# A two-block model on one core: the steps round the recurrences' gates and between states, values and first scores in another order

## The chip, the core and the metric

The kernel runs on one core of a Trainium2 chip. A core has TensorE (matmuls into PSUM; its weight loads are shown apart), VectorE, ScalarE, GpSimd and SyncE, each with a queue of its own that it works off in order, and shares of 16 DMA engines. Here SyncE only issues transfers; ScalarE and GpSimd issue some too. The metric is the device time of one execution in microseconds, as the median of several runs.

## The reference

Two model blocks are applied to x of shape (1, 512, 1024), all in fp32.

```
first block:   h = rmsnorm(x);  p = h @ w_in -> lru_x, lru_gate, four_in
               c = depthwise conv of lru_x over time
               two gated linear recurrences over c (forward, backward):
                 a = exp(8 r log_sigmoid(lam)),  h_t = a_t h_(t-1) + sqrt(1-a^2) i c
               y = concat(gelu(lru_gate) * (h_f + h_b), fft2 of four_in)
               x = x + y @ w_out
               x = x + expert-choice MoE(rmsnorm(x)): 16 experts, 64 rows each, FF 2048
               x = rmsnorm(x)
second block:  h = rmsnorm(x);  h @ w_in -> q, k, v, z_a, u, z_s, g_a, g_s
               y_a = (banded attention with relative bias(q, k, v) * silu(z_a)) @ w_attn_out
               y_s = diagonal state space model of u, 32 groups, 64 states each;
                     gelu, GLU, * silu(z_s), @ w_ssm_out
               x = rmsnorm(x + (sigmoid(g_a) * y_a + sigmoid(g_s) * y_s) @ w_out)
```

## The kernel before

The order of all instructions is written out by hand: each engine runs its instructions in the order in which the code issues them, and semaphores make it wait for operands and for buffers. Most matmuls take fp32 operands as a pair of a rounded high part and a low part: `Pair.put` (lines 107 and 108, or 110 and 111 with a scale) copies the high part on ScalarE and subtracts it on VectorE or GpSimd, and `mm3` (lines 121 to 123) runs high by high, high by low, low by high. A projection of one weight unit is 24 matmuls.

The dense weights come in units of 512 KB through `Stream`: `load` (line 140) has SyncE fetch a unit into half of one of two raw buffers, `work` splits it into one of three pair buffers, with the low part on GpSimd or, for every third unit, on VectorE, and then calls `load` again; `get` hands out a unit and works ahead so that two more lie split. A raw buffer holds a pair of units, so a load into it waits until both of its units have been split. SyncE's queue is worked in order, so what is issued behind such a load waits too.

First block, start. SyncE loads xT (x transposed) in five transfers, the first two weight units, x in four blocks `xs`, two more units, a table of constants with the identity, the gate weights `bd`, the DFT table, and two further units. `half` and `part` split the first two units and xT's eight parts. `two` holds the projections of unit 0 and 1, and a third `in_proj` follows. The row norm is applied late: ScalarE squares the four x blocks with a running sum (line 344), `inv_sqrt` (lines 210 to 221) turns sums into row scales `rt`, VectorE multiplies the identity by them into `dg` (line 348, four blocks), and TensorE spreads them over the partitions by a matmul with ones (line 360). The result `rr` (line 362) multiplies each projection. Beside that, VectorE does a series of tiny steps on 8 columns (lines 327 to 341) for the logarithm of the decay, `ls`, `nls` and `ls2`, which `decay` uses much later. Then come convolution, gates (`gates`, line 376), recurrences, the Fourier half, and the output projection.

Experts. The weights of 16 experts, 1 MB a transfer, stream through ring buffers whose first loads are issued near the end of the first block.

Second block. Projections of q and k alternate with the state space model in four quarters: `chunk_inputs`, `chunk_scan` (VectorE scans), `chunk_states` (VectorE, GpSimd for line 1253, VectorE for the write of `Hs` in line 1254), `chunk_outputs` (lines 1266 and 1267, TensorE, then a copy to `Y`), `turn_outputs` (transposes in line 1275 and copies to `Yc`). `values` projects v in four weight units into four PSUM banks (`vp`), which line 1311 scales and copies to `vt`. Yc goes to memory as `ys` in eight stores (line 1313) and comes back as `yc` (line 1409) after the heads. The biases' table `bt` takes U's place, is loaded by ScalarE's queue, has the far bias subtracted and a mask written on GpSimd. `att` takes Hs's place and holds the split of one head's q and k; its unused halves are set to zero on GpSimd. Each head then runs: eight score matmuls (lines 1371 and 1372), bias and maximum on VectorE (1374, 1376), Exp on ScalarE, the next head's split, `fill` twice, transposes of the probabilities (1393), `fill` once; each second head adds the value matmuls (1405). `fill` is one of 24 projections for the gates; with 23 inside the heads, the last one runs after them (`fill(24)`). Behind it the attention's output is multiplied by `za` (1416), split as `yap`, and projected by `thin`.

Of the kernel before, what the change touches and what calls it, by code (L numbers as in the profile page):

```python
# [21 lines left out]
S = 512  # L22
# [38 lines left out]
def body(ctx, tc, a, out, dbg=None):  # L61
# [30 lines left out]
    def P(n, lo=0, hi=None):  # L92
        b, e = PP[n]
        return pp[:, b + lo:(e if hi is None else b + hi)]
# [108 lines left out]
    def inv_sqrt(pool, ss, tag, y=None):  # L203

        return [r for r in inv_sqrt_steps(pool, ss, tag, y)][1]
# [22 lines left out]
    with ExitStack() as c1:  # L228
# [5 lines left out]
        with ExitStack() as ca:  # L234
# [13 lines left out]
            for d in range(2, DB, 2):  # L248
                SP.dma_start(xT0[:, d:d + 2], a["xT"][:, d:d + 2])
            for tb in range(TB):  # L250
                SP.dma_start(xs[:, tb, :], a["x"][tb * 128:(tb + 1) * 128, :])
                if tb == 1:
                    ws.load()
            SP.dma_start(cst, a["cst"][:, 0:CCK])
            ws.load()
# [24 lines left out]
            for _ in range(12):  # L280
                PE.matmul(p[:, 0:128], ones, ones, start=True, stop=True)

# [8 lines left out]
            def half(i, j, eng):  # L291
                u, t = w[i]
                u.put((slice(None), slice(j * 512, j * 512 + 512)), t[:, j * 512:j * 512 + 512], eng)

            def part(d):
                hT.put((slice(None), d), xT0[:, d], DVE, scale=P("n1", d, d + 1))

            half(0, 0, DVE)
# [7 lines left out]
            for d in range(4, DB):  # L306
                part(d)
# [6 lines left out]
            ws.work(DVE)  # L314

            ls = ta.tile([128, 8], F32, name="ls")
            nls = ta.tile([128, 8], F32, name="nls")
            ls2 = ta.tile([128, 8], F32, name="ls2")
            l_in = ta.tile([128, 8], F32, name="l_in")
            DVE.tensor_copy(l_in[:, 0:4], P("lamf"))  # L320
            DVE.tensor_copy(l_in[:, 4:8], P("lamb"))
            ey = ta.tile([128, 8], F32, name="ey")
            act(ey, l_in, AF.Abs)
            act(ey, ey, AF.Exp, scale=-1.0)
# [9 lines left out]
            for q in (15, 13, 11, 9, 7, 5, 3, 1):  # L334
                DVE.tensor_mul(acc, acc, s2)
                DVE.tensor_scalar(acc, acc, 1.0 / q, None, op0=OP.add)
            DVE.tensor_mul(acc, acc, sv)
# [4 lines left out]
            act(rt, rt, AF.Sqrt)  # L342
            for tb in range(TB):
                act(early[:, 0:2].rearrange("p a b -> p (a b)"), xs[:, tb, :], AF.Square, accum_out=ss[:, tb:tb + 1])
            inv_sqrt(ta, ss, "n1", rt)
            dg = early2[:, 1]
            for tb in range(TB):
                DVE.tensor_scalar(dg[:, tb * 128:(tb + 1) * 128], ident, rt[:, tb:tb + 1], None, op0=OP.mult)
# [854 lines left out]
    def stile(tag, shape, name):  # L1203
        return spool.tile(shape, F32, name=name, tag="ssm_" + tag)
# [96 lines left out]
    for q in range(3):  # L1301
        chunk_outputs(q)
    values(1)
    values(2)
    Yc = stile("cos", [128, 32, 64], "Yc")
    chunk_outputs(3)
    values(3)
    for q in range(4):
        turn_outputs(q)
    for tb in range(TB):  # L1310
        act(vt[:, tb, :], vp[tb], AF.Copy, scale=stat[:, 7, tb:tb + 1])
    for tau in range(8):
        SP.dma_start(ys[:, tau, :].rearrange("(g c) n -> c g n", c=16), Yc[tau * 16:(tau + 1) * 16])

    bt = ta2.tile([128, 8, 256], F32, name="bt", tag="U")
    ACT.dma_start(bt, bass.AP(tensor=a["rel"].tensor, offset=a["rel"].offset, ap=[[1, 128], [384, 8], [1, 256]]))
    POOL.tensor_tensor(bt, bt, bfar[:, :, None].to_broadcast([128, 8, 256]), op=OP.subtract)
    POOL.memset(bt[0:64, :, 0:64], -1e30)
# [3 lines left out]
    for i in range(2):  # L1322
        POOL.memset(kl[i][(1 - i) * 64:(1 - i) * 64 + 64].bitcast(F32), 0.0)

# [11 lines left out]
    split_head(0)  # L1336

# [3 lines left out]
    zs = stile("cos", [128, 4, S], "zs")  # L1341
    ga = stile("W", [128, 8, S], "ga")
    big = stile("BM", [128, 4, 2048], "big")
    gs = big[:, 2:4].rearrange("p a (b s) -> p (a b) s", s=S)
# [3 lines left out]
    def fill(n=1):  # L1348
        for _ in range(n):
            i = nfill[0]  # L1350
            nfill[0] += 1
            if i >= 24:
                return
            p = scratch("fl")
            DVE.tensor_tensor(p, proj(), rr, op=OP.mult)
            if i < 4:
                act(za[:, i, :], p, AF.Silu)
            elif i < 8:
                act(zs[:, i - 4, :], p, AF.Silu)
            else:  # L1360
                act((ga if i < 16 else gs)[:, (i - 8) % 8, :], p, AF.Sigmoid, bias=P("gb", i - 8, i - 7))

    for hp in range(4):
# [76 lines left out]
    for b in range(4):  # L1440
        w = ws.get()
        pb = thin(w, 128, yg)
        sgb = scratch("sgb")
        act(sgb, pb, AF.Sigmoid, bias=P("bglu", 4 + b, 5 + b))
        if b:
            ysp.put((slice(None), b - 1), last, DVE)
        pa = thin(w, 0, yg)
        yz = scratch("yz")
        DVE.scalar_tensor_tensor(yz, pa, P("bglu", b, b + 1), sgb, op0=OP.add, op1=OP.mult)
        DVE.tensor_mul(yz, yz, zs[:, b, :])  # L1450
        last = yz
# [188 lines left out]
```

## Time and profile before

| | us |
|---|---|
| median of 3 runs | 1538.53 |
| lowest and highest of them | 1536.11, 1540.04 |
| profiled execution, its time | 1536.9 |
| its span, first to last instruction | 1535.1 |
| TensorE busy in the span | 1457.6 |
| VectorE, ScalarE, GpSimd busy | 607.4, 403.1, 184.0 |
| mean granted clock of TensorE, of 1 | 0.983 |

Starts and durations are microseconds from the start of the span. In rows PE is TensorE, PEld its weight loads, DVE VectorE, ACT ScalarE, POOL GpSimd, SP SyncE; a q behind it is the queue that issues transfers. L12 is line 12 of the kernel before. A row of the timeline shows start, duration, engine, line, operation, output<-inputs, shapes and count; in brackets stands how long the engine had been idle before it, and what released it. TensorE's busy time is modelled and its matmuls overlap, so its pace is read from the distance of starts.

### The profile page before, as it was taken

What the parts mean: (1) busy time and instruction counts of PE and PEld (TensorE: products, weight loads), DVE (VectorE), ACT (ScalarE), POOL (GpSimd) and SP (SyncE); (2) the same over time, 40 slices, a digit from 0 to 9 for tenths busy, and PEclk for the clock granted to TensorE, in tenths of its full rate; (3) what the DMA queues carried; (4) which work ended last, traced back from release to release, by engine and by line L of the source; (5) the groups of instructions that cost most, each with busy time, mean ns of one, the idle gap of its engine ahead of it and who ended that gap; (6) DMA issues with size and microseconds to landing.
All of it is one profiled execution on the core that took longest, in us unless ns stands there. A gap on an engine that the chain in (4) does not pass through costs nothing. (4 is left out here: it accounts for less than half of the span.)

```text
span 1535.1 us, 17258 instructions
## 1 busy us (share of the span) xinstructions
PE 1457.6 (95%) x6822; PEld 805.3 (52%) x6822; DVE 607.4 (40%) x1279; ACT 403.1 (26%) x690; POOL 184.0 (12%) x125
## 2 busy tenths in 40 slices
PE   7999899999999999999999999899999879999997
PEld 6778633333333334444334343343477757877886
DVE  6773512221222243333333332531354525554454
ACT  5654211100100121000100100210263146655533
POOL 2323000000001000000000001000022322113352
PEclk8999899999999999999999999999999989999999
DMA  7116989999999999999999999999927131222231
GB/s 276 55 55 264 371 331 407 426 428 426 427 427 417 426 426 426 427 427 426 427 426 427 427 428 406 413 421 427 382 87 137 56 101 65 83 83 94 99 124 55
DMA packets 88753, 461.77 MB, mean 301 GB/s; under 512 B 16670, under 2 KB 26270, under 8 KB 40416
## 3 DMA queue, kind: packets, MB, share of 16 engines
q1 hardware_dynamic: 86112, 456.14, 73.4%
q10 hardware_dynamic: 1904, 2.80, 0.6%
q0 software_dynamic: 656, 1.71, 0.4%
q8 instruction: 54, 0.88, 0.2%
q14 instruction: 27, 0.22, 0.0%
HBM read 455.25 MB, written 4.19 MB: 299 GB/s over the span
## 5 line engine op out<-in xcount | busy, mean ns | idle before, releaser
L1062 PE MATMUL gu<-w,xT 128*64 128x512 f32 x2032 | 471.8, 596 | 11.2 <-DMA w<-in_w_up_dram 9.9
L1062 PEld LDWEIGHTS gu<-w,xT 128*64 128x64 f32 x2032 | 167.5, 137 | 278.9 <-issue 229.5
L1085 PE MATMUL dn<-w,sh 128*64 128x512 f32 x944 | 217.4, 597 | 0.0
L962 DVE TENSOR_TENSOR xs<-tp,xs 128x512 f32<-128x512 f32 x120 | 77.5, 687 | 276.1 <-PE tp L960 276.1
L121 PE MATMUL ps<-hTh,w 128*128 128x512 f32 x384 | 156.1, 406 | 3.3 <-ACT hTh L110 1.8
L108 POOL TENSOR_TENSOR w<-w 128x1024 fp32r<-128x1024 f32 (+1 forms) x51 | 121.9, 2395 | 283.1 <-ACT w L107 247.8
L122 PE MATMUL ps<-hTl,w 128*128 128x512 f32 x384 | 153.8, 400 | 0.3 <-DVE hTl L111 0.3
L123 PE MATMUL ps<-hTh,w 128*128 128x512 f32 x384 | 153.2, 399 | 0.0
L1085 PEld LDWEIGHTS dn<-w,sh 128*64 128x64 f32 x944 | 63.7, 137 | 115.4 <-issue 115.0
L1042 ACT ACTIVATE sh<-gu 128x512 f32<-128x512 f32 x32 | 19.1, 597 | 396.5 <-PE gu L1062 394.7
L107 ACT ACTIVATE w<-w 128x1024 fp32r<-128x1024 f32 (+1 forms) x82 | 84.1, 1032 | 73.9 <-PE ps L123 43.5
L121 PEld LDWEIGHTS ps<-hTh,w 128*128 128x128 f32 x384 | 73.4, 191 | 22.5 <-issue 3.8
L122 PEld LDWEIGHTS ps<-hTl,w 128*128 128x128 f32 x384 | 73.7, 192 | 17.9 <-DVE hTl L111 0.6
L123 PEld LDWEIGHTS ps<-hTh,w 128*128 128x128 f32 x384 | 73.7, 192 | 17.6
L960 PE MATMUL tp<-Y,GT 128*128 128x512 f32 x240 | 72.3, 422 | 0.4 <-ACT ssm_BM L850 0.4
L108 DVE TENSOR_TENSOR w<-w 128x1024 fp32r<-128x1024 f32 (+1 forms) x31 | 39.5, 1277 | 73.4 <-ACT w L107 73.4
L960 PEld LDWEIGHTS tp<-Y,GT 128*128 128x128 f32 x240 | 40.1, 188 | 52.1 <-issue 44.6
L1044 DVE COPY sh<-gu 128x512 f32<-128x512 f32 x32 | 22.1, 691 | 105.6 <-PE gu L1062 71.5
L861 POOL DMA_DIRECT2D ssm_BM<-raw x8 | 4.2, 538 | 459.8 <-DVE raw L857 459.8
L929 ACT ACTIVATE xin<-tp 128x512 f32<-128x512 f32 x16 | 9.6, 597 | 188.7 <-PE tp L924 188.7
L935 DVE TENSOR_TENSOR xT<-tp,pp 128x512 f32<-128x512 f32 x16 | 11.1, 692 | 118.2 <-PE tp L933 118.2
L1049 PE MATMUL tp<-cst,sh 128*128 128x128 f32 x256 | 38.9, 285 | 17.0 <-DVE sh L1057 11.5
(441 smaller groups left out, 1769.9 us busy)
## 6 DMA issues: line engine op xcount, KB each, us to landing
w<-in_w_gate_dram SPq DMA_DIRECT2D x127, 1024.0 KB, 13.3
w<-in_w_up_dram SPq DMA_DIRECT2D x127, 1024.0 KB, 14.1
w<-in_w_down_dram SPq DMA_DIRECT2D x118, 1024.0 KB, 14.8
w<-in_w_dram SPq DMA_DIRECT2D x80, 512.0 KB, 4.3
w<-in_w_down_dram SPq DMA_DIRECT2D x16, 512.0 KB, 8.1
xs<-in_x_dram SPq DMA_DIRECT2D x4, 512.0 KB, 9.5
h2n<-in_w_down_dram SPq DMA_DIRECT2D x2, 1024.0 KB, 19.3
out_dram<-ga SPq DMA_DIRECT2D x8, 256.0 KB, 2.0
```

The lines of the kernel that those rows point to most:

```text
L107: act(h, src, AF.Copy)
L108: eng.tensor_tensor(l, src, h.bitcast(F32), op=OP.subtract)
L121: PE.matmul(p, x[0], y[0], start=start, stop=False)
L122: PE.matmul(p, x[0], y[1], start=False, stop=False)
L123: PE.matmul(p, x[1], y[0], start=False, stop=stop)
L960: PE.matmul(p, GT[e][:, tb * 128:(tb + 1) * 128], Yt[e][h * 512, 512][i], start=(i == 0), stop=(i == 1))
L962: DVE.tensor_add(sl, p, sl)
L1042: act(o, i, AF.Copy)
L1044: DVE.tensor_copy(o, i)
L1049: PE.transpose(p[:, j * 128:(j + 1) * 128], gus[n][:, j * 128:(j + 1) * 128], ident)
L1062: PE.matmul(gu[n][j * 64:j * 64 + 64], xt[:, d, :], wt[kind, e, d][:, n * 512:(n + 1) * 512], start=(d == 0), stop=(d == DB - 1))
L1085: PE.matmul(dn[n][j * 64:j * 64 + 64], hTe[:, k + 8 * j, :], w[:, j * 1024 + n * 512:j * 1024 + n * 512 + 512], start=(k == 0), stop=(k == 7))
```

## The change

Start of the first block: x's blocks are loaded between the pairs of xT instead of behind them; weight units 2 and 3 are both loaded behind the constants (unit 2 stood between x's second and third block before). Sixteen warming matmuls are run instead of twelve. The Abs and Exp for the decay move ahead of the splits. The squares and the square root that loads its table move between the last four xT parts on ScalarE. Row scales and diagonal are computed before the last five steps of the decay, no longer after them. Unit 2's low part goes to GpSimd instead of VectorE.

Second block: the outputs of the third quarter move behind values(1). The biases' table is issued by GpSimd, right behind the last quarter's outputs, and the zeroing of `att` is put ahead of the subtraction. Head 0's split moves ahead of values(3). `vt` is copied on ScalarE and VectorE by turns. One `fill` runs before the transposes of the outputs and the stores of `ys`, so that all 24 now lie before the end of the heads. `zs` is allocated at its first use.

```diff
-            for d in range(2, DB, 2):
-                SP.dma_start(xT0[:, d:d + 2], a["xT"][:, d:d + 2])
             for tb in range(TB):
                 SP.dma_start(xs[:, tb, :], a["x"][tb * 128:(tb + 1) * 128, :])
-                if tb == 1:
-                    ws.load()
+                d = 2 * tb + 2
+                if d < DB:
+                    SP.dma_start(xT0[:, d:d + 2], a["xT"][:, d:d + 2])
             SP.dma_start(cst, a["cst"][:, 0:CCK])
-            ws.load()
+            ws.load(2)
...
-            for _ in range(12):
+            for _ in range(16):
                 PE.matmul(p[:, 0:128], ones, ones, start=True, stop=True)
...
+            def squares(tb):
+                act(early[:, 0:2].rearrange("p a b -> p (a b)"), xs[:, tb, :], AF.Square, accum_out=ss[:, tb:tb + 1])
...
-            for d in range(4, DB):
-                part(d)
+            part(4)
+            squares(0)
+            part(5)
+            act(rt, rt, AF.Sqrt)
+            part(6)
+            squares(1)
+            part(7)
+            squares(2)
+            squares(3)
...
             ws.load(2)
-            ws.work(DVE)
+            ws.work(POOL)
...
                 DVE.tensor_scalar(acc, acc, 1.0 / q, None, op0=OP.add)
+            inv_sqrt(ta, ss, "n1", rt)
+            dg = early2[:, 1]
+            for tb in range(TB):
+                DVE.tensor_scalar(dg[:, tb * 128:(tb + 1) * 128], ident, rt[:, tb:tb + 1], None, op0=OP.mult)
             DVE.tensor_mul(acc, acc, sv)
...
             DVE.tensor_scalar(ls2, ls, 2.0, None, op0=OP.mult)
-            act(rt, rt, AF.Sqrt)
-            for tb in range(TB):
-                act(early[:, 0:2].rearrange("p a b -> p (a b)"), xs[:, tb, :], AF.Square, accum_out=ss[:, tb:tb + 1])
-            inv_sqrt(ta, ss, "n1", rt)
-            dg = early2[:, 1]
-            for tb in range(TB):
-                DVE.tensor_scalar(dg[:, tb * 128:(tb + 1) * 128], ident, rt[:, tb:tb + 1], None, op0=OP.mult)
             ws.work(POOL)
...
-    for q in range(3):
+    for q in range(2):
         chunk_outputs(q)
     values(1)
+    chunk_outputs(2)
     values(2)
     Yc = stile("cos", [128, 32, 64], "Yc")
     chunk_outputs(3)
-    values(3)
-    for q in range(4):
-        turn_outputs(q)
-    for tb in range(TB):
-        act(vt[:, tb, :], vp[tb], AF.Copy, scale=stat[:, 7, tb:tb + 1])
-    for tau in range(8):
-        SP.dma_start(ys[:, tau, :].rearrange("(g c) n -> c g n", c=16), Yc[tau * 16:(tau + 1) * 16])
 
     bt = ta2.tile([128, 8, 256], F32, name="bt", tag="U")
-    ACT.dma_start(bt, ...)
-    POOL.tensor_tensor(bt, bt, bfar[:, :, None].to_broadcast([128, 8, 256]), op=OP.subtract)
-    POOL.memset(bt[0:64, :, 0:64], -1e30)
+    POOL.dma_start(bt, ...)
...
         POOL.memset(kl[i][(1 - i) * 64:(1 - i) * 64 + 64].bitcast(F32), 0.0)
+    POOL.tensor_tensor(bt, bt, bfar[:, :, None].to_broadcast([128, 8, 256]), op=OP.subtract)
+    POOL.memset(bt[0:64, :, 0:64], -1e30)
...
     split_head(0)
+    values(3)
+    for tb in range(TB):
+        r = stat[:, 7, tb:tb + 1]
+        if tb % 2:
+            DVE.tensor_scalar(vt[:, tb, :], vp[tb], r, None, op0=OP.mult)
+        else:
+            act(vt[:, tb, :], vp[tb], AF.Copy, scale=r)
...
-    zs = stile("cos", [128, 4, S], "zs")
+    zs = []
...
             elif i < 8:
-                act(zs[:, i - 4, :], p, AF.Silu)
+                if i == 4:
+                    zs.append(stile("cos", [128, 4, S], "zs"))
+                act(zs[0][:, i - 4, :], p, AF.Silu)
...
+    fill()
+    for q in range(4):
+        turn_outputs(q)
+    for tau in range(8):
+        SP.dma_start(ys[:, tau, :].rearrange("(g c) n -> c g n", c=16), Yc[tau * 16:(tau + 1) * 16])
     for hp in range(4):
```

## Rows read from the trace of the kernel before

**Rows 1.** The page's 40 slices of the span: busy tenths of the DMA engines.

```profile
DMA  7116989999999999999999999999927131222231
```

**Rows 2.** Timeline of TensorE, third quarter's outputs to head 0's transposes.

```profile
1213.54 0.48 PE L1267 MATMUL ps<-ssm_W,Hs 128*64 128x128 f32 x1 [4.86 <-DVE Hs L1254]
...
1216.82 0.50 PE L121 MATMUL ps<-w,hTh 128*128 128x512 f32 x1
...
1228.18 0.45 PE L1266 MATMUL ps<-ssm_BM,U 128*64 128x128 f32 x4
...
1235.81 1.91 PE L1275 MATMUL ps<-cst,y 128*128 128x128 f32 x16
...
1249.44 0.58 PE L1372 MATMUL ps<-att 128*128 128x256 f32 x1 [6.28 <-POOL att L1323]
...
1263.91 1.25 PE L1393 MATMUL ps<-cst,pr 128*128 128x128 f32 x10
```

**Rows 3.** Windows: length; busy (instructions) PE, PEld, DVE, ACT, POOL; granted clock; DMA.

```profile
114.00:117.00 3.00, 3.00 (x8) 2.31 (x7) 2.30 (x5) 1.85 (x4) 0.18 (x1) 0.50 0.00 0
1213.00:1217.00 4.00, 3.46 (x31) 3.29 (x32) 3.00 (x4) 0.61 (x2) 0.81 (x1) 0.57 0.02 4
1249.00:1252.00 3.00, 2.56 (x8) 2.37 (x9) 1.84 (x6) 1.24 (x1) 0.90 (x2) 0.50 0.00 0
```

**Rows 4.** Timelines of VectorE and GpSimd in the second block.

```profile
1191.63 2.85 DVE L1254 TENSOR_TENSOR Hs<-gq,t 128x504 f32<-128x504 f32 x1 [1.39 <-POOL gq L1253]
...
1244.63 3.60 POOL L1317 TENSOR_TENSOR bt<-bt,bfar 128x2048 f32<-128x2048 f32 x1 [18.28 <-DMA bt<-in_rel_dram]
```

**Rows 5.** Transfers by queue: count, KB each, median us from issue to landing.

```profile
bt<-in_rel_dram ACTq DMA_DIRECT2D x1, 1024.0 KB, 6.7
...
raw<-in_ssm_dram POOLq DMA_DIRECT2D x1, 512.0 KB, 5.4
...
ssm_BM<-raw POOLq DMA_DIRECT2D x1, 256.0 KB, 14.0
```

**Rows 6.** Timelines of ScalarE and VectorE behind the last head.

```profile
1408.80 0.60 ACT L1407 ACTIVATE qk<-ps 128x512 f32<-128x512 f32 x1 [0.86 <-PE ps L1405]
...
1410.04 2.49 DVE L108 TENSOR_TENSOR yapl<-qk,yaph 128x512 fp32r<-128x512 f32 x4
```

**Rows 7.** TensorE in the first block: one row of its timeline, two of its waits.

```profile
31.44 2.07 PE L360 MATMUL ps<-early 128*128 128x512 f32 x2 [4.86 <-DVE early L348]
...
PE ps L121 <- ACT h2n L376: 3.6, 1, 3.6
...
PE ps L121 <- DVE early L487: 1.5, 1, 1.5
```

**Rows 8.** ScalarE's first 25 us: timeline, and the squares as a group.

```profile
9.39 0.72 ACT L110 ACTIVATE hTh<-h2n,pp 128x512 fp32r<-128x512 f32 x1 [0.63 <-DMA h2n<-in_xT_dram]
...
11.67 2.55 ACT L110 ACTIVATE hTh<-h2n,pp 128x512 fp32r<-128x512 f32 x4
...
15.74 1.06 ACT L107 ACTIVATE w<-w 128x1024 fp32r<-128x1024 f32 x1 [1.52 <-DMA w<-in_w_dram]
...
18.71 1.28 ACT L342 ACT_TABLE_LOAD   x1
...
L344 ACT ACTIVATE early<-xs x4: 1043/1060/1061, 20.1 to 23.6; 128x1024 f32<-128x1024 f32 x4
```

**Rows 9.** VectorE and GpSimd, 18 to 32 us: decay steps (first, last), row scales, diagonal.

```profile
18.72 0.17 DVE L327 TENSOR_SCALAR sv<-ey 128x8 f32<-128x8 f32 x1 [0.52 <-ACT ey L324]
...
22.83 0.17 DVE L336 TENSOR_SCALAR acc<-acc 128x8 f32<-128x8 f32 x1
...
24.83 0.17 DVE L210 TENSOR_SCALAR v_n<-ss 128x4 f32<-128x4 f32 x1 [1.06 <-ACT early L344]
...
26.28 5.11 DVE L348 TENSOR_SCALAR early<-cst,rt 128x128 f32<-128x128 f32 x4
...
26.27 4.64 POOL L108 TENSOR_TENSOR w<-w 128x1024 fp32r<-128x1024 f32 x2 [12.52 <-DVE rt L221]
```

More of the change, by code (lines that the diff above doesn't have):

```diff
@@ L279, in body @@
             p = bank()
-            for _ in range(12):
+            for _ in range(16):
                 PE.matmul(p[:, 0:128], ones, ones, start=True, stop=True)
+            ls = ta.tile([128, 8], F32, name="ls")
+            nls = ta.tile([128, 8], F32, name="nls")
+            ls2 = ta.tile([128, 8], F32, name="ls2")
+            l_in = ta.tile([128, 8], F32, name="l_in")
+            DVE.tensor_copy(l_in[:, 0:4], P("lamf"))
+            DVE.tensor_copy(l_in[:, 4:8], P("lamb"))
+            ey = ta.tile([128, 8], F32, name="ey")
+            act(ey, l_in, AF.Abs)
+            act(ey, ey, AF.Exp, scale=-1.0)
             w = []
@@ L313, in body @@
             ws.load(2)
-            ws.work(DVE)
[L316 to L324, printed above, removed]
+            ws.work(POOL)
             sv = ta.tile([128, 8], F32, name="sv")
@@ L1306, in body @@
     chunk_outputs(3)
-    values(3)
-    for q in range(4):
-        turn_outputs(q)
-    for tb in range(TB):
-        act(vt[:, tb, :], vp[tb], AF.Copy, scale=stat[:, 7, tb:tb + 1])
-    for tau in range(8):
-        SP.dma_start(ys[:, tau, :].rearrange("(g c) n -> c g n", c=16), Yc[tau * 16:(tau + 1) * 16])
     bt = ta2.tile([128, 8, 256], F32, name="bt", tag="U")
-    ACT.dma_start(bt, bass.AP(tensor=a["rel"].tensor, offset=a["rel"].offset, ap=[[1, 128], [384, 8], [1, 256]]))
-    POOL.tensor_tensor(bt, bt, bfar[:, :, None].to_broadcast([128, 8, 256]), op=OP.subtract)
-    POOL.memset(bt[0:64, :, 0:64], -1e30)
+    POOL.dma_start(bt, bass.AP(tensor=a["rel"].tensor, offset=a["rel"].offset, ap=[[1, 128], [384, 8], [1, 256]]))
     att = tq.tile([128, 4, S], F32R, name="att", tag="Hs")
@@ L1449, in body @@
         DVE.scalar_tensor_tensor(yz, pa, P("bglu", b, b + 1), sgb, op0=OP.add, op1=OP.mult)
-        DVE.tensor_mul(yz, yz, zs[:, b, :])
+        DVE.tensor_mul(yz, yz, zs[0][:, b, :])
         last = yz
```

## The prediction

> **What bounds the kernel now.** I read the table of slices first, then TensorE's own timeline round the two places that the diff touches, then the timelines of the engines that it waits for there. The slices say what a moved step can be worth: the transfers run at nine tenths or more from about the fourth to the twenty-eighth slice (the experts) and near one tenth before and after [rows 1]. So the experts' stage lives on weights whose loads are issued as the first block ends, and a shift of that end moves everything behind it. The second half has transfers to spare, and its limit must be an engine.
>
> The timeline of TensorE between states and scores shows which. It waits 4.86 us until the states of the third quarter are written, then runs the outputs slowly; the transposes of the outputs end at 1235.81 + 1.91 = 1237.72, and the scores get going only at 1249.44 [rows 2]. Behind either pause it was granted half speed: 0.57 in the mean of 1213 to 1217, 0.50 from 1249 to 1252 [rows 3]. Nothing of that is work. The other touched place is at 31.44, where the broadcast matmul of line 360 waits 4.86 us for the diagonal of row scales [rows 7].
>
> **The change from states to first scores.** The matmuls are the same, so I lay them end to end with times from the rows. A values unit of 24 matmuls takes (1228.18 - 1216.82) / 2 = 5.68 us, the outputs of a quarter 1235.81 - 1216.82 - 3 x 5.68 = 1.95, the transposes 1.91 [rows 2]; a `fill` has the 24 matmuls of a values unit, 5.68. The eight score matmuls took 2.56 us at half speed, so 1.28 at full [rows 3]. The first two quarters' outputs end at about 1208.7 - 0.3 = 1208.4 (the 4.86 us run back from 1213.54, less two matmuls that go ahead of the wait).
>
> New order: values(1) to 1214.1, outputs(2) 1216.0, values(2) 1221.7, outputs(3) 1223.7, values(3) 1229.4, the first fill 1235.0, transposes 1236.9, scores of head 0 1238.2, two fills 1249.6. There head 0's probabilities are turned, which before began at 1263.91 [rows 2]: 14.3 us earlier, and with one more fill done (5.68). Together 20.0 us.
>
> Is every step ready? The third quarter's states are written at 1213.5, before outputs(2) at 1214.1. The fourth quarter's: the weight split of the last values unit now reaches GpSimd right behind its part of the states, and VectorE's write of the states will lie under it, as at 1191.63, where the same write took 2.85 us [rows 4]; from about 1217.5 that is 1220.4, and outputs(3) start at 1221.7. Head 0's split follows outputs(3) on ScalarE and VectorE and is through by about 1227, where before it sat behind all value evictions. The memsets of `att` are no longer behind the table, so line 1372 doesn't wait for it.
>
> The biases' table: its issue waits on GpSimd's queue for U, which outputs(3) still read, so it goes at 1223.7; behind it are queued the two memsets, the 3.60 us subtraction of line 1317 [rows 4] and the split of a later fill's weight. Landing is not shown for this transfer from this queue. Bounds: 6.7 us as issued by ScalarE; 5.4 for half the bytes from GpSimd; 14.0 for the last of eight from GpSimd under the experts' traffic [rows 5]. It is nearest the first two in surroundings (transfers mostly idle), so I take 7: landed 1231, ready 1235, and VectorE wants it for scores at 1237. At 14 it is ready at 1241.8, and the weight split behind it at 1244.2, for a fill at 1243.9: about nothing to 1 us, or 3 with a slow clock behind it.
>
> SyncE: the stores of `ys` now stand behind a weight load that waits until both units of its pair are split, some 10 us after the scores begin. By my estimate from ScalarE's order they land near 1259; `zs`, which takes Yc's place, is first written near 1263 (two fills, transposes and a fill, scores and a fill behind 1238.2), and yc is read more than 100 us later. I cost this at nothing; the margin is 4 us. The silu of the first fill adds one table load on ScalarE, under TensorE's fill.
>
> The cover taken away: before, one fill was left behind the heads and ran while the last head's output went through copy, product and split. Now the attention's output projection meets that chain bare. The copy starts at 1408.80, the splits on VectorE run 1410.04 to 1412.53 [rows 6], about 0.62 each. The first matmul can start near 1409.9, its second at 1410.7; from there the twelve run through. Loss 1.9 us. If the projection had to wait for the whole split, 3.8. Whether the clock falls here: behind a wait of 1.5 us it fell to half and stayed there for over 3 us [rows 3, 7], costing about 1.7; here two waits of 1.2 and 0.6 follow each other. I take half of it: 2.7, between 1.9 and 5.5.
>
> **The change in the first block.** The squares of x move ahead of unit 2's weight copy on ScalarE; x's blocks are put between those of xT; unit 2's low part goes from VectorE to GpSimd. Between the first xT pair's use at 9.39 and unit 2's at 15.74 lie five transfers of 512 KB, 1.27 us each [rows 8]. New landings: first xT pair 10.7, second 13.2, third 15.7, last x 17.0, unit 2 18.7. From 13.2 on ScalarE has four xT parts (2.55), four squares at (23.6 - 20.1) / 3 = 1.17, and a table load with a square root (1.5) [rows 8]: through at 21.9, unit 2's copy to 23.0, GpSimd's half 2.3 more (4.64 for two [rows 9]): 25.3. The third projection can thus end at 25.3 + 22 x 0.237 = 30.5 at the earliest; before, it ended 4.86 us ahead of 31.44. That alone still fits in front of 31.44.
>
> But the diagonal also needs VectorE. ScalarE does the last xT part before two squares, by 19.5, VectorE's half follows to 20.3; then come 21 small steps for the recurrences' decay, 18.72 to 23.0 before [rows 9], only now in front of the row scales. At 23.0, with 13 of them done, GpSimd takes unit 2's split. The trace shows such pairs excluding each other: four diagonal blocks took 5.11 us beside two splits of 4.64 [rows 9], and the states 2.85 [rows 4]. So eight steps are left at 25.3 and end at 26.9; the row scales 1.4 (24.83 to 26.28 [rows 9]) make 28.4, and there ScalarE has copied the next weight and GpSimd starts as VectorE does, as at 26.27: 5.1 more, 33.5. Against 31.44 that is 2.1 us later. If the small steps run freely, 31.1, and TensorE, not having paused, runs line 360 at full speed: 1.3 us earlier. If the four blocks lose to a third split too: 4.5 later.
>
> The Trainium skill ("SBUF — State Buffer", section "Who interferes with whom") speaks against this move: a VectorE instruction with two SBUF inputs, or a scalar operation in a two-port mode, and a GpSimd one that reads SBUF block each other whole, and the first to start wins. By it the small steps are held, 2.1 us lost; without it 0.3 to 1.3 are gained. The rows above agree with it for large tiles; none shows tiles of 8 columns.
>
> I take 1.9 lost, near the held case since both kinds of row were held, a little less for the chance that TensorE's pause gets too short for the clock to fall. It is not absorbed: between here and the experts TensorE waits 3.6 us for ScalarE's sigmoids [rows 7], which hang on the same chain from the row scales, and the experts' loads start when that ends. The four more warming matmuls and the earlier Abs and Exp stand where both engines wait for the first weights anyway, and cost nothing.
>
> **Sum.** -20.0 + 2.7 + 1.9 = -15.4 us. On the profiled execution, 1536.9 us (span 1535.1 and 1.8 round it), that is 1521.5; its time is 1.6 under the median of 1538.53, so the median goes to 1523.1, said as 1523.
>
> **Rivals.**
> Held nowhere in the first block: the squares' earlier place pays, -1.3 in place of +1.9: 1520. For it: line 360 is gated by the diagonal alone [rows 7], and squares end 3 us earlier. Against: the 21 steps in front.
> A new wait eats part: the projection waits for the whole split with a slow clock (5.5 for 2.7), or the table or `zs` comes late (3), and the diagonal loses thrice (4.5 for 1.9): 1526 to 1531. For it: the 4 us margin and the untested queue.
> The change doesn't do what it says: the scores wait for the table all the same, through GpSimd's queue or shared buffers, and only the 4.86 us wait with its 1.4 us of slow clock goes, less 4.6 given back: 1537, no change. Against: the memsets come ahead of line 1317 in that queue, and the scores' matmuls don't read the table.
> Slower than before, by one mechanism: GpSimd's table transfer. Each us by which it lands behind about 1238.5 delays the weight split queued behind it and a fill with it. All 15.4 us are used up if it lands at 1254, 30 us from its issue; the longest row is 14.0 [rows 5]. The Trainium skill ("SBUF — State Buffer", section "SBUF: two separate sides") says that VectorE in a two-port mode locks GpSimd out of writing descriptors; no run here shows it.
>
> **Chances and range.** Forecast 0.55; first block gains 0.15; a new wait 0.20; no effect 0.05; slower 0.05. A repeat of this kernel moves by 0.3%, 4.6 us, so the first three cases count as faster, 0.90. The range reaches from the first rival less the spread of the three runs shown (1520 less 4, 1516) to the new waits (1530).
>
> **What would show it.** Right: TensorE without a pause over 1 us from the first quarter's outputs to the last head, granted 1.0 throughout; a pause of one to two us before the attention's projection; line 360 one to three us later and VectorE's small steps held about 2.4 us at one point; sums of the expert stage as before. Wrong: line 1372 or 1374 waiting for `bt`, a fill waiting for GpSimd's split, ScalarE's `zs` waiting for `ys`, or the first block's end unmoved.

## The result and the profile after

The changed kernel took 1520.03 us in the median of four runs (1515.99 to 1523.59), the kernel before 1537.32 beside it. The ratio is 0.9888, with a 95% interval from 0.9854 to 0.9921; 1523 was forecast, in a range from 1516 to 1530. A second set of runs gave 0.9875 (0.9854 to 0.9896). The profiled execution took 1518.64 us with a span of 1516.8; the one before had 1536.9 and 1535.1, so 18.3 us of span are gone, where the sum said 15.4.

TensorE's timeline through the second block, in the new order: values(1), outputs(2), values(2), outputs(3), values(3), the first fill, the outputs' transposes, the first scores, head 0's transposes.

```profile
1208.41 0.50 PE L121 MATMUL ps<-w,hTh 128*128 128x512 f32 x1
...
1214.18 0.45 PE L1272 MATMUL ps<-ssm_BM,U 128*64 128x128 f32 x4
...
1216.13 0.50 PE L121 MATMUL ps<-w,hTh 128*128 128x512 f32 x1
...
1221.91 0.34 PE L1272 MATMUL ps<-ssm_BM,U 128*64 128x128 f32 x2
...
1223.86 0.50 PE L121 MATMUL ps<-w,hTh 128*128 128x512 f32 x1
...
1229.54 0.40 PE L121 MATMUL ps<-hTh,w 128*128 128x512 f32 x1
...
1235.13 1.91 PE L1281 MATMUL ps<-cst,y 128*128 128x128 f32 x16
...
1236.79 0.36 PE L1385 MATMUL ps<-att 128*128 128x256 f32 x1
...
1249.32 1.25 PE L1407 MATMUL ps<-cst,pr 128*128 128x128 f32 x10
```

Nothing in this list has a bracket: neither the 4.86 us in front of the third quarter's outputs nor the 6.28 us in front of the scores is left [rows 2]. A third wait of the kernel before is gone too: its first score matmul waited for head 0's split on ScalarE.

```profile
1242.57 0.58 PE L1371 MATMUL ps<-att 128*128 128x256 f32 x1 [4.86 <-ACT att L1333]
```

Head 0's transposes start at 1249.3; 1249.6 was forecast. The granted clock of the same stretches, which was 0.57 and 0.50 [rows 3] (columns as there):

```profile
1213.00:1217.00 4.00, 4.00 (x42) 3.20 (x41) 2.97 (x4) 2.24 (x4) 0.84 (x1) 1.00 0.00 0
1249.00:1252.00 3.00, 3.00 (x20) 2.60 (x19) 1.51 (x4) 1.76 (x4) 0.00 (x0) 1.00 1.02 264
```

TensorE's waits of over 0.2 us from 1130 to the end: engine and line, what is waited for, us in total, times, longest.

```profile
PE ps L121 <- ACT yaph L107: 1.2, 1, 1.2
PE ps L122 <- DVE yapl L108: 0.3, 1, 0.3
PE ps L1241 <- ACT st L1233: 0.3, 1, 0.3
```

The first two are the new pause behind the last head: the attention's projection meets the copy and the splits bare [rows 6]. GpSimd's timeline round the biases' table [rows 4]:

```profile
1224.19 0.95 POOL L1316 DMA_DIRECT2D bt<-in_rel_dram  x1 [1.59 <-PE ps L1273]
1225.18 1.09 POOL L1321 MEMSET att<- 64x512 f32 x2
1232.00 3.60 POOL L1322 TENSOR_TENSOR bt<-bt,bfar 128x2048 f32<-128x2048 f32 x1 [5.73 <-DMA bt<-in_rel_dram]
1235.66 0.52 POOL L1323 MEMSET bt<- 64x512 f32 x1
1236.15 2.38 POOL L108 TENSOR_TENSOR w<-w 128x1024 fp32r<-128x1024 f32 x1
```

The transfer's landing is where the third row starts its subtraction, 7.8 us behind the issue's start (7 taken). VectorE's write of the last states lies under GpSimd's splits and takes 2.87 us, as taken from the row of 2.85 [rows 4]:

```profile
1217.48 2.87 DVE L1260 TENSOR_TENSOR Hs<-gq,t 128x504 f32<-128x504 f32 x1 [1.47 <-POOL gq L1259]
```

In the first block, VectorE's timeline shows one decay step of 128 x 8 numbers that takes 2.27 us where its neighbours take 0.17 [rows 9], and the diagonal's four blocks:

```profile
22.71 2.27 DVE L344 TENSOR_TENSOR acc<-acc,s 128x8 f32<-128x8 f32 x1
...
27.56 0.16 DVE L221 TENSOR_TENSOR rt<-rt,t_n 128x4 f32<-128x4 f32 x1
27.76 5.17 DVE L349 TENSOR_SCALAR early<-cst,rt 128x128 f32<-128x128 f32 x4
```

GpSimd's timeline beside it:

```profile
22.59 2.37 POOL L108 TENSOR_TENSOR w<-w 128x1024 fp32r<-128x1024 f32 x1 [7.61 <-ACT w L107]
27.74 4.71 POOL L108 TENSOR_TENSOR w<-w 128x1024 fp32r<-128x1024 f32 x2 [2.78 <-DVE rt L221]
```

And TensorE's broadcast matmul, 31.44 before [rows 7]:

```profile
32.98 1.45 PE L366 MATMUL ps<-early 128*128 128x512 f32 x2 [2.57 <-DVE early L349]
```

Each long row on VectorE begins up to 0.12 us behind a split of GpSimd (or two of them) and ends with it or up to 0.5 us later. The broadcast comes 1.5 us later; 2.1 was forecast. But at 71 us both kernels stand at the same time, at 1208 too, and all of the 18.3 us come after that. Where the first block's lateness went was the main question for the experiments.

### The profile page after: what moved, and what is told of

Its sections match the earlier page's. It is cut to its first block, busy times and chain, and to the rows that moved or that the text cites. A ratio compares the mean times of both kernels' runs of the same rounds, so it can differ in the third digit from the quotient of the medians.

```text
span 1516.8 us, 17276 instructions
## 1 busy us (share of the span) xinstructions
PE 1455.0 (96%) x6830; PEld 803.0 (53%) x6830; DVE 611.9 (40%) x1280; ACT 402.7 (27%) x689; POOL 188.1 (12%) x127
## 4 chain that ended last, share of the span: by engine, by line
PE 77%; DMA 10%; DVE 7%; ACT 3%; issue 2%; POOL 1%; SPq 0%; ACTq 0%; POOLq 0%; DVEq 0%
PE gu L1068 25%; PE dn L1091 13%; DMA w<-in_w_up_dram 9%; PE ps L121 7%; PE ps L122 7%; PE ps L123 7%; PE tp L930 4%; PE tp L966 3%; PE tp L1055 2%; DVE cT L396 1%; PE dn L1114 1%; ACT sh L1048 1%; PE tp L955 1%; PE ps L1419 1%; PE ps L1407 1%
## 5 line engine op out<-in xcount | busy, mean ns | idle before, releaser
L123 PEld LDWEIGHTS ps<-hTh,w 128*128 128x128 f32 x384 | 72.6, 189 | 18.1 <-POOL w L108 1.3
L1050 DVE COPY sh<-gu 128x512 f32<-128x512 f32 x32 | 22.1, 690 | 105.1 <-PE gu L1068 70.5
```

The source lines that it names most:

```text
L123: PE.matmul(p, x[1], y[0], start=False, stop=stop)
```

## The experiments

A span of one and the same kernel moves by several us from run to run, so most effects are read at fixed instructions. The table gives, of each profiled execution, the start of the broadcast matmul, of the first product with the row scales (VectorE, `uT`), of ScalarE's table loads for the gelu ("123") and for the row scales at the block's end ("148"), of the copy of the first outputs (L1275, "1210"), the time from there to the end of the span, and the granted clock in two windows (112 to 122 and 1070 to 1100). Each row is one trace. From "steps behind" on, the kernels have a single run each, but for "outputs first" and "both", which have four.

| kernel | broadcast | uT | 123 | 148 | 1210 | to the end | clock 112:122 | clock 1070:1100 |
|---|---|---|---|---|---|---|---|---|
| before | 31.44 | 34.18 | 123.01 | 149.25 | 1210.11 | 325.0 | 0.83 | 0.95 |
| second part only | 31.63 | 34.37 | 123.17 | 149.38 | 1212.32 | 306.9 | 0.83 | 0.88 |
| changed | 32.98 | 35.10 | 122.97 | 147.92 | 1210.05 | 306.7 | 1.00 | 0.89 |
| changed, again | 32.74 | 35.25 | 123.56 | 149.81 | 1214.20 | 306.7 | 0.83 | 0.91 |
| first part only | 33.05 | 35.04 | 122.94 | 147.88 | 1206.22 | 326.4 | 1.00 | 1.00 |
| steps behind | 30.99 | 35.80 | 123.82 | 148.77 | 1211.36 | 306.8 | 1.00 | 0.89 |
| split by VectorE | 34.34 | 37.08 | 125.72 | 150.67 | 1209.55 | 306.7 | 1.00 | 1.00 |
| a fill behind | 33.05 | 34.85 | 123.15 | 149.91 | 1212.04 | 304.9 | 0.83 | 0.90 |
| no early fill | 32.90 | 34.70 | 122.97 | 149.72 | 1212.58 | 305.0 | 0.83 | 0.89 |
| outputs first | 32.88 | 34.67 | 123.00 | 149.74 | 1212.61 | 313.3 | 0.83 | 0.89 |
| table by ScalarE | 32.85 | 34.64 | 122.97 | 149.22 | 1212.43 | 306.8 | 0.83 | 0.89 |
| diagonal by ScalarE | 30.39 | 32.08 | 121.31 | 146.24 | 1205.68 | 306.7 | 1.00 | 0.94 |
| table late | 32.96 | 35.30 | 124.81 | 151.56 | 1213.19 | 307.7 | 0.83 | 0.92 |
| both | 30.38 | 32.07 | 122.20 | 148.44 | 1212.60 | 304.9 | 0.83 | 0.88 |

**Each part alone.** The kernel before with only the edits from `for q in range(3)` on ("second part only"), and with only those ahead of it ("first part only").

> The kernel before, with the changes between states, values and first scores alone; its first block is as before. Theory (all of the gain is made there, and the first block's shift is absorbed by about 71 us of the span): 18.3 us off the kernel before, near 1519, and the interval of its ratio holds that of the changed kernel; head 0's transposes some 14 us earlier as in the changed kernel, a pause of 1.2 and 0.3 us behind the heads, and line 360's matmul back at 31.4. Rival (the 1.5 us by which the first block's broadcast matmul came later are lost for the whole kernel): 19.8 us off, 1517.5. Second rival (the first block's new order gains through TensorE's clock, which kept its full level there in the changed kernel): 17.0 us off, 1520.3.

Measured: 1521.79 us (1520.28 to 1525.12) against 1539.21, ratio 0.9903 (0.9879 to 0.9927). From 1210 to the end it took 306.9 us, as the changed kernel does: the gain lies there. 19.8 us off is outside the interval; 17.0 and 18.3 can't be told apart by the time.

> The kernel before, with the first block's changes alone. Theory (absorbed): within 0.5 us of the kernel before at 1150 us of the span and at the end, whatever line 360's matmul does; that matmul starts near 33.0, behind a step of VectorE held for about 2.3 us by GpSimd's weight split. Rival (not absorbed): 1.5 us slower at the end. Second rival (the clock): 1.3 us faster at the end, with a granted clock of 1.00 where the kernel before has 0.50 at 114 to 117.

Measured: ratio 0.9994 (0.9982 to 1.0006), so between 2.8 us faster and 0.9 slower, which excludes the forecast 1.9. The broadcast and the held step were as expected, but in this one trace the block ended 1.4 us earlier, with a clock of 1.00 at 112 to 122; at 1150 it was 3.9 us ahead, not within 0.5. Neither lead belongs to the order of the instructions: see "The changed kernel again" below and the last section. From 1210 to the end, where its code is that of the kernel before, it took 1.4 us more than that kernel. The wait for the states is the same there (4.88 us); the clock behind it was not. From 1213 to 1217 it was granted 0.77; in the four us that correspond, 1217 to 1221, the kernel before had 1.00. So the gain behind 1210 is 18.1 to 18.3 us against the one trace of the old order and up to 19.7 against the other.

**What the held step is worth.** First, the decay's steps behind the diagonal ("steps behind"):

```
+inv_sqrt(ta, ss, "n1", rt)
+dg = early2[:, 1]
+for tb in range(TB):
+    DVE.tensor_scalar(dg[:, tb * 128:(tb + 1) * 128], ident, rt[:, tb:tb + 1], None, op0=OP.mult)
 sv = ta.tile([128, 8], F32, name="sv")
 ...
-inv_sqrt(ta, ss, "n1", rt)
-dg = ...
```

> The changed kernel with VectorE's small steps for the recurrences' decay put behind the four diagonal blocks, as their last operations are already. Theory: the row scales no longer wait for 21 small steps, so the diagonal is through 3 to 5 us earlier than at 32.9 and the broadcast matmul starts where the third projection ends, near 30.5 to 31; but the sigmoids' stretch on ScalarE and the first gates take the gain up, so that at 71 us of the span, and at the end, it stands within 0.5 us of the changed kernel. Rival (the first block's end hangs on the diagonal): 2 us faster at 71, at 130 and at the end.

Measured: one run, 1519.98 us. The broadcast was ready at 30.99, as expected, but VectorE then had 26 small steps between the diagonal and `uT`, which came 0.7 us later than in the changed kernel. That lateness wasn't absorbed: at 123 and at 148 it is still 0.85. VectorE's timeline shows what happened to the row scales:

```profile
22.98 2.14 DVE L217 TENSOR_TENSOR t_n<-rt 128x4 f32<-128x4 f32 x1
25.15 2.31 DVE L219 TENSOR_TENSOR t_n<-t_n,v_n 128x4 f32<-128x4 f32 x1
27.50 2.33 DVE L220 TENSOR_SCALAR t_n<-t_n 128x4 f32<-128x4 f32 x1
...
30.06 0.88 DVE L338 TENSOR_SCALAR early<-cst,rt 128x128 f32<-128x128 f32 x4
```

GpSimd's timeline beside it:

```profile
22.71 7.08 POOL L108 TENSOR_TENSOR w<-w 128x1024 fp32r<-128x1024 f32 x3 [7.61 <-ACT w L107]
```

Three splits of GpSimd, and three instructions of VectorE on 4 columns that each last as long as one split. As soon as GpSimd is idle, the four diagonal blocks take 0.88 us, not 5.17.

Second, unit 2's low part on VectorE again ("split by VectorE"):

```
-ws.work(POOL)
+ws.work(DVE)
```

> The changed kernel with the low part of the first stream's unit 2 split by VectorE again, not by GpSimd. Theory (the two engines exclude each other even for tiles of 8 columns): no small step of VectorE is longer than 0.2 us any more, where the changed kernel has one of 2.27; VectorE has 1.2 us for the split in its place, so the diagonal is through about 1.0 us earlier, and the end is unmoved within 0.5 us. Rival (the 2.27 us step had another cause, such as a late operand): the long step stays.

Measured: one run, 1518.12 us. No long step was left among the small ones, so the cause is the split. But the diagonal came 1.4 us later, not 1.0 earlier. VectorE's timeline tells why:

```profile
22.41 1.23 DVE L108 TENSOR_TENSOR w<-w 128x1024 fp32r<-128x1024 f32 x1 [2.42 <-ACT w L107]
23.56 0.17 DVE L336 TENSOR_SCALAR sv<-ey 128x8 f32<-128x8 f32 x1
...
29.18 5.10 DVE L349 TENSOR_SCALAR early<-cst,rt 128x128 f32<-128x128 f32 x4
```

The split stands ahead of the steps in VectorE's queue and waits for ScalarE's copy until 22.41; in the changed kernel the steps begin at 20.04 and half of them are done by then. I had forgotten that wait. The edit that I had charged with 2.3 us for the hold is worth 1.4 us against the order without it (at the diagonal, in one trace each). And again nothing is absorbed: 1.98 us at `uT` are 2.75 at 123 and at 148.

**The cover behind the heads.** One fill less in the first head, so that one of the 24 is left behind the last ("a fill behind"):

```
-fill(2 if h < 7 else 1)
+fill(2 if 0 < h < 7 else 1)
```

> The changed kernel with one fill, not two, between the first head's scores and the turning of its probabilities, so that one of the 24 fills is left behind the last head again. Theory: the probabilities of head 0 are ready at 1242.8 in the changed kernel and the remaining fill ends near 1243.9, so nothing waits there, and the pause of 1.2 and 0.3 us behind the heads goes: from the first outputs (1210) to the end of the span 1.9 us less. Rival (the first head's chain doesn't fit under one fill, with two table loads of ScalarE and two splits of the second head in it): a pause of 1 to 3 us ahead of head 0's transposes, and nothing gained or a loss up to 1 us.

Measured: 306.7 us to the end became 304.9, so 1.8 us less, and the waits at `yaph` and `yapl` are gone; no wait appeared in the first head.

**Does the table gate the scores?** No fill ahead of the outputs' transposes ("no early fill"), so that one goes behind the heads here too:

```
-fill()
 for q in range(4):
     turn_outputs(q)
```

> The changed kernel without the fill ahead of the outputs' transposes; it goes behind the last head. The first scores come at about 1231.4, some 5 us before the biases' table is ready (1236.2). Theory: TensorE's scores don't read the table; VectorE's addition waits for it until 1236.2, the probabilities are ready near 1241.7 and the two fills end near 1244, so nothing is lost there and 1.9 us are gained from 1210 to the end. Rival (the table gates the scores all the same, through GpSimd's queue with the weight split behind the table, or through PSUM): TensorE waits 2 us or more in the first head, and the end is 0 to 4 us later than in the changed kernel.

Measured: 305.0 to the end, 1.7 less. VectorE's timeline shows that its addition waits for the table, and it alone does:

```profile
1238.16 0.30 DVE L1387 TENSOR_TENSOR ps<-ps,bt 128x128 f32<-128x128 f32 x1 [5.17 <-POOL bt L1323]
```

TensorE has no wait over 0.3 us from 1130 to the end in this run. The scores start at 1233.70, 4.5 us ahead of the table, and the two fills behind them hide it. So the early fill isn't needed for the scores' pause to go. By the rows of the kernel before, that pause was two waits, one for head 0's split and one for `att`'s memsets, which stood behind the table; no run moves only one of the two.

**The third quarter's outputs ahead of values(1) again** ("outputs first"):

```
-for q in range(2):
+for q in range(3):
     chunk_outputs(q)
 values(1)
-chunk_outputs(2)
```

> The changed kernel with the third quarter's outputs ahead of the second values unit again, the rest as changed. Theory: the wait of 4.86 us for the states comes back near 1208.5, TensorE goes at half speed for some 3 us behind it, and everything from there on, head 0's transposes included, is 6 to 6.3 us later: near 1526. Rival (the wait is only moved, since the values unit then hides what follows): 3 us or less.

Measured: 1526.63 us, ratio 0.9917 (0.9892 to 0.9942). To the end it took 313.3 us, 6.6 more than the changed kernel. TensorE's timeline and the windows behind the wait:

```profile
1216.04 0.32 PE L1273 MATMUL ps<-ssm_W,Hs 128*64 128x128 f32 x1 [4.86 <-DVE Hs L1260]
```

```profile
1215.00:1218.00 3.00, 1.96 (x22) 1.96 (x24) 2.65 (x4) 0.60 (x1) 0.27 (x1) 0.75 0.02 5
1218.00:1222.00 4.00, 4.00 (x23) 3.17 (x20) 1.22 (x2) 1.55 (x2) 2.18 (x2) 0.76 0.00 0
```

The wait itself and 1.7 us of slow clock behind it.

**Who issues the table** ("table by ScalarE"):

```
-POOL.dma_start(bt, ...)
+ACT.dma_start(bt, ...)
```

> The changed kernel with the biases' table issued by ScalarE again, from its new place. Theory (the place matters, the issuing engine doesn't): the issue follows ScalarE's copy of the last quarter's outputs near 1224, the table lands within 1 us of the changed kernel's 1232, and from 1210 to the end nothing moves by more than 0.3 us. Rival (GpSimd's own issue is worth something, as it frees ScalarE's queue, or costs its 0.95 us): 0.5 to 2 us either way behind 1236.

Measured: 306.8 to the end against 306.7. The transfer took 5.4 us from issue to landing, against 7.6 from GpSimd, and nothing waits for the difference.

**What a late table costs** ("table late"): four memsets of it on GpSimd ahead of its transfer:

```
+for _ in range(4):
+    POOL.memset(bt, 0.0)
 POOL.dma_start(bt, ...)
```

> The changed kernel with four additional memsets of the whole table on GpSimd ahead of the table's transfer, some 8 to 9 us by four times the 0.52 of a quarter of it each, so that it lands near 1240.5 and is ready near 1244.7. Theory (the price of the slower rival): the weight split queued behind the table ends near 1247.1 where the third fill wants it at 1243.9, so TensorE waits some 3 us ahead of that fill, with half speed behind it, and the end is 3 to 6 us later from 1210 on. Rival (the table has more slack than that, since the scores don't read it): no wait of TensorE over 1 us and under 1 us lost.

Measured: 307.7 to the end, 1.0 us lost; the expected 3 to 6 were too many. GpSimd's timeline:

```profile
1227.06 7.42 POOL L1317 MEMSET bt<- 128x2048 f32 x4 [1.31 <-PE ps L1273]
...
1240.88 3.60 POOL L1324 TENSOR_TENSOR bt<-bt,bfar 128x2048 f32<-128x2048 f32 x1 [4.01 <-DMA bt<-in_rel_dram]
1244.54 0.52 POOL L1325 MEMSET bt<- 64x512 f32 x1
1245.02 2.40 POOL L108 TENSOR_TENSOR w<-w 128x1024 fp32r<-128x1024 f32 x1
```

This run stands 3.1 us behind the changed kernel at 1210, the four memsets took 7.4 us, not 8 to 9, and the transfer landed 1.7 us faster (5.9 against 7.6). So on the changed kernel's scale the table landed at 1237.7 and the split behind it ended at 1244.3, 0.5 us behind the start of the third fill (1243.75), which wants it; TensorE waits 0.4 us there for this split. The mechanism is the one described, but my numbers for the delay were off, and the point from which it costs lies near 1237, not at the prediction's 1238.5.

**The diagonal on ScalarE** ("diagonal by ScalarE"):

```
-DVE.tensor_scalar(dg[:, tb * 128:(tb + 1) * 128], ident, rt[:, tb:tb + 1], None, op0=OP.mult)
+act(dg[:, tb * 128:(tb + 1) * 128], ident, AF.Copy, scale=rt[:, tb:tb + 1])
```

> The changed kernel with the four diagonal blocks of row scales made by ScalarE, each a copy scaled by a column, and not by VectorE; ScalarE's next two weight copies, and with them GpSimd's splits, come behind them. Theory: the diagonal takes about 1.3 us instead of 5.17, so it is through by 29.3; the broadcast matmul follows the third projection at 30.5 to 31 without a pause of over 0.5 us, and the shift is carried: the first product with the row scales some 2.5 to 3 us earlier than 35.1, and the block's end at 130 to 154 by 2 to 3 us, if TensorE's clock falls nowhere else. Rival (slack of ScalarE's sigmoids absorbs what comes before them): the broadcast comes earlier, but at 71 us all is as in the changed kernel.

Measured: one run, 1514.21 us. ScalarE's four blocks:

```profile
27.90 1.28 ACT L349 ACTIVATE early<-cst,rt 128x128 f32<-128x128 f32 x4 [1.04 <-DVE rt L221]
```

The broadcast then follows the third projection at 30.39 with no wait, and `uT` starts at 32.08, 3.0 us earlier than in the changed kernel. ScalarE's weight copies stand behind the blocks now, so GpSimd's next split began only at 30.21. The run therefore shows the diagonal and the splits one after the other; that ScalarE's blocks would run freely beside a split isn't shown, and with GpSimd idle VectorE needed 0.88 us for them ("steps behind"). At 123 and 148, 1.7 us of the lead are left, so the slack of the rival doesn't take it. Of the rest, 1.1 us went where GpSimd's split of `bd` now lies beside more of VectorE's three steps for `cT`: these took 5.48 us in place of 4.37.

**Both** together, the diagonal by ScalarE and a fill behind the heads:

> The changed kernel with the diagonal made by ScalarE and one fill left behind the last head, together. Theory: 1.9 us off from 1210 to the end, and 2.0 to 3.6 us off at 154, of which what is left at 1070 to 1130 depends on TensorE's granted clock there: 3.5 to 5.5 us under the changed kernel, near 1516 in the median, against 1520. Rival (the first block's lead is lost at the experts' transfers or to the clock): only the 1.9 us behind the heads, 1518.

Measured: 1517.26 us (1512.44 to 1519.36), ratio to before 0.9853 (0.9835 to 0.9871). The changed kernel on the same chip had 1522.51 and 0.9875 (0.9854 to 0.9896): the intervals overlap. 304.9 us to the end are 1.8 less; of the first block's lead, 1.4 us were left at 148 against the changed kernel beside it, where 2.0 to 3.6 were expected. Whether these 1.4 reach the end isn't shown: from 148 to 1210 this run took 1064.2 us, the longest of the 14 traces, whose shortest is 1058.3.

**The changed kernel again.**

> The changed kernel itself, beside the others on the same chip, with more rounds. Theory (TensorE's clock behind the same short waits, at 114 and 1070 to 1100 of the span, isn't decided by the order of the instructions): its granted clock at 114 to 116 is 1.00 in one run and 0.5 in another, and the spans of one and the same kernel differ by 2 to 4 us for that alone; median near 1520. Rival (the changed first block keeps the clock up by itself): 1.00 at 114 to 116 again.

Measured: five runs from 1514.69 to 1522.80, median 1522.51. The windows at 114, first of the first run of the changed kernel:

```profile
114.00:116.00 2.00, 2.00 (x10) 1.64 (x9) 1.30 (x4) 0.89 (x2) 0.00 (x0) 1.00 0.00 0
```

then of this one:

```profile
114.00:116.00 2.00, 2.00 (x8) 1.51 (x8) 1.36 (x3) 0.85 (x3) 0.00 (x0) 0.73 0.00 0
```

and of "table by ScalarE", whose first block has the same code:

```profile
114.00:116.00 2.00, 2.00 (x6) 1.54 (x5) 1.30 (x4) 0.88 (x2) 0.00 (x0) 0.50 0.00 0
```

In all three the wait in front, for `early`, is 1.49 or 1.50 us and ends within 0.7 us of the same time. The order of the instructions doesn't decide what the clock does there. The eight traces with the changed first block pass 148 at 149.47 in the mean (147.88 to 151.56), the two with the old one at 149.32.

## Why the prediction was right, point by point

**The second block** was forecast at 20.0 us and gave 20.2: head 0's transposes come 39.27 us behind the first outputs' copy (1249.32 - 1210.05) instead of 53.80, which is 14.5 (14.3 forecast), and one more fill of 5.7 us is done by then. The row-by-row walk held within 0.3 us at each station but the table, 1 us late with 5 us of slack. That the gain is made here and here alone, "second part only" shows. "Outputs first" shows that 6.6 of it are the wait for the states (4.86) and the slow clock behind it. The other 13.6 lie at head 0: two waits of 4.86 and 6.28 in the kernel before and about 2.5 of slow clock behind them (0.50 from 1249 to 1252 [rows 3], 0.76 from 1252 to 1256). The 1.28 us that the prediction took for the scores came from a window that ends at 1252 and holds seven of the eight, and one matmul of the fill; the changed kernel's eight take 1.39 (1236.79 to 1238.18), so little hangs on it. The rival in which the scores wait for the table is refuted by "no early fill". The one in which GpSimd's table makes the kernel slower needed a landing at 1254, 22 us later than the one measured; "table late" shows the point from which it would begin. The term put at nothing for `ys` held: its last store was issued at 1252.9, the slowest took 7.4 us to land, and ScalarE first writes `zs` at 1265.17 with no wait for it.

**The cover behind the heads** was a term of 2.7, a mean between two cases for the clock. Measured: 20.2 - 18.3 = 1.9, the lower bound, with the two waits of 1.2 and 0.3 and no fall of the clock (1.00 from 1395 to 1400). "A fill behind" gets 1.8 of it back.

**The first block** is the term that was mis-sized: 1.9 us lost were taken, about none was measured. The mechanism behind it, that GpSimd's split holds a small step of VectorE, was right to 0.1 us (2.27 against 2.3). The rule of the Trainium skill ("SBUF — State Buffer", "Who interferes with whom") that spoke against the move is borne out here for tiles of 8 and of 4 columns. The size was not right. The broadcast came 1.4 us late in the mean over the eight traces (32.93 against 31.54), not 2.1; `uT` 0.7 (34.94 against 34.28), and at 123 it is 0.2 (123.30 against 123.09), most of it from "table late", whose clock fell once more (0.57 from 88 to 92); without that trace nothing is left. The whole part measures between 2.8 us faster and 0.9 slower. One of the prediction's signs of being wrong came true with that, the first block's end unmoved: 149.47 at 148 against 149.32.

Two give-backs show in the rows. TensorE no longer pauses for 4.86 us but for 2.57, and its broadcast matmul took 2.07 us before [rows 7], at half speed (0.50 from 32 to 34), and 1.12 to 1.84 since. The prediction took only 0.2 us off for the chance that the clock doesn't fall there. It fell behind this pause in four of the eight traces, the changed kernel's first among them, and not in the other four. The windows, first of the changed kernel, then of "no early fill":

```profile
34.00:36.00 2.00, 2.00 (x6) 1.40 (x5) 0.90 (x2) 0.77 (x2) 0.00 (x0) 0.50 0.08 33
34.00:36.00 2.00, 2.00 (x11) 1.59 (x10) 1.29 (x2) 1.17 (x2) 0.00 (x0) 1.00 0.11 43
```

And VectorE's first steps for `cT` start 0.36 us behind `uT` where they started 0.78 behind it before and 0.79 in "split by VectorE", the one other order of the first block with a pause of 5 us; what they wait for there isn't shown. In the four traces without a fall, where the broadcast took 1.12 or 1.13 ("a fill behind", "no early fill", "outputs first", "table by ScalarE"), `uT` was 0.5 to 0.7 late against the kernel before, and at 41 us at most 0.2 of it was left. In the first trace of the changed kernel 0.4 us were left at 41, and they went between 66 and 71, with a granted clock of 1.00 at 62 to 70 where the kernel before had 0.79. That no slack swallows the shift up to the block's end is right all the same: 0.7, 1.98 and -3.0 us at `uT` came out at 148 as 0.85, 2.75 and -1.7. I had said in my expectations, after the first trace, that ScalarE's sigmoids absorb it; "steps behind" and "split by VectorE" refute that. That a shift of the block's end moves everything behind it, as the prediction has it, isn't shown: from 148 to 1210 the traces differ by 5.9 us, more than any of these shifts.

**The sum** said -15.4 and the first profiled spans differ by 18.3: 0.2 more in the second block, 0.8 at the heads, and the 1.9 of the first block. The median of all runs moved by 17.3. It came out at 1520, the number of the first rival ("held nowhere"), but not by that mechanism: the small step was held for 2.27 us. One kernel moves by 8 us from run to run, so the time alone doesn't tell 1520 from 1523.

## What to carry to other kernels

A pause of TensorE that is only order, not work, can be costed by laying the matmuls end to end and asking of each whether its inputs are ready; that sum held to 0.3 us over 40 us. A hold between two engines should be costed against what stands in its place, queue and waits included, not against an idle engine; and if a short chain of small steps lies between two of the other engine's long instructions, a third engine may do it (1.28 us on ScalarE for 5.17), where what then comes later has its price too (1.1 us at `cT`). Where one and the same kernel moves by 8 us from run to run, time effects of 2 us from a fixed instruction to a fixed instruction, over several traces.

## What the runs showed of the hardware that was not expected

Three instructions of VectorE on 128 x 4 numbers took 2.14, 2.31 and 2.33 us, each beside one split of GpSimd: the hold is paid per instruction of VectorE, so while GpSimd's instructions follow one another without a gap, a chain of small dependent steps can lose one whole GpSimd instruction at each.

The same wait of TensorE, of 1.50 us at 113, was followed by a granted clock of 1.00, 0.73 or 0.50 in runs with the same code, worth 1.3 to 1.8 us at 148. The last expert does the same at two places of the window from 1070 to 1100. The first lies behind four small matmuls (L975, 1.98 us). The sixteen matmuls after them, in the changed kernel and then in "first part only":

```profile
1074.48 5.35 PE L1068 MATMUL gu<-w,xT 128*64 128x512 f32 x16
1073.16 3.65 PE L1068 MATMUL gu<-w,xT 128*64 128x512 f32 x16
```

The granted clock from 1074 to 1078 was 0.59 in the first and 1.00 in the second. The other place lies behind a wait of 2.0 us that TensorE has in every run there, for VectorE's `sh` (L1050): the changed kernel had 0.70 from 1094 to 1097, "first part only" 1.00. The latter's lead was 1.3 us at L975, 3.0 when that wait ended and 3.9 soon behind it, so about 2.6 of the 3.8 by which it is ahead at 1210 are the clock's. All 14 traces have the same code in this stretch; the clock fell at the first place in ten of the traces and at the second in twelve. What decides wasn't found.
